# Stick-breaking scan kept as the remaining product, with a floor tile as its mask, and joint transfers for the heads' operands

## The chip, the cores and the metric

The kernel runs on one core of one Trainium2 chip. TensorE (PE) multiplies matrices and transposes, VectorE (DVE) and ScalarE (ACT) work on whole tiles, GpSimd (POOL) and SyncE (SP) mostly issue transfers (DMAs); each engine works through its own instructions in program order. The metric is device time of one execution in microseconds (us), the median of several timed runs.

## What is computed

One decoder block: three gated attention branches side by side (stick-breaking, forgetting, memory cross-attention), merged, projected and added to the input, then a squared-ReLU MLP. Sequence 1024, width 1024, 8 + 8 heads of 64 and 4 memory heads of 128, all in float32. The change is about the stick-breaking branch:

```python
z = jnp.einsum('bhtd,bhsd->bhts', q[:, :, q0:kend], k[:, :, :kend]) * scale
strict = s_idx < t_idx
log_rem = jnp.where(strict, jax.nn.log_sigmoid(-z), 0.0)
after = lax.cumsum(log_rem, axis=3, reverse=True) - log_rem
w = jnp.where(strict, jnp.exp(jax.nn.log_sigmoid(z) + after), 0.0)
outs.append(jnp.einsum('bhts,bhsd->bhtd', w, v[:, :, :kend]))
```

Read from the newest key to the oldest, each key takes the share sigmoid(z) of what is left of a stick, and leaves sigmoid(-z) of it. The weight of key s is what is left before s minus what is left after it. So the sum over keys of weight times value can be written with "what is left" itself and with differences of neighbouring values (`value_step` makes these).

## The kernel before

**Stages.** By the profiled run: up to about 470 us the input is normed and most of the input projection is done; from about 470 to 860 us the attention of all branches runs, with the remaining gate projections and the first of the branch output products put between its pieces on TensorE; the merge, the output projection and the MLP follow (L1871 and on). Every float32 matmul is split in two parts: a high part (a copy on ACT to a shorter format) and a low part (the difference, on DVE), and three products of these are summed.

**What sets the order.** Up to the end of attention the program is written by a planner that runs when the program is built: `Machine` (L184) steps through generators that ask for an engine (`Op`, with a cost in us), a buffer (`Get`) or an event, and writes an engine's next instruction when that engine is free in the plan. So a changed cost or a changed number of buffers moves instructions on all engines. `late` values break ties, and `side` work (the projections) fills TensorE when no attention piece is ready. On the chip each engine keeps the written order, whatever its real durations are.

**Stick-breaking tiles.** `sb_tile` (L812) takes one head and one block of 128 queries, in chunks of up to 512 keys. A chunk gets a buffer `rho` and a PSUM bank, TensorE makes the scores, DVE adds a large number above the diagonal (L834, last chunk only), ACT takes two sigmoids from the scores (L827 into `rho`, L828 into `beta`), and DVE scans from the newest key to the oldest with state = rho * state + beta, which leaves one minus the remaining product (L843). Chunks of the same row wait for the newer one. The queries carry the sign -1 (L1537), so sigmoid(scale * score) is sigmoid(-z). The four `rho` buffers are two tiles of pool `RR`, which has three, lent until the last stick-breaking pair is over (L1609 to L1611, `whole_again`); memory attention and the loads of branch outputs take their tiles from `RR` too.

**Units.** `unit` (L888) runs two such query blocks, then transposes their weights by blocks of 256 keys (`turn`, L917), copies the high part (`pth`, L922, ACT), subtracts for the low part (`ptl`, L924, DVE) and multiplies by the values (L934). Forgetting heads (`fox_tile`, L854) take scores (L869, L870), row maxima (L874) and exponentials (L885) in place of the scan.

**Operands of the heads.** `load_pairs` (L984) fetches queries and keys of two heads at a time from DRAM through POOL's queue, per head and half of the sequence. A stick-breaking head needs its high keys twice, in partitions 0 to 63 and 64 to 127 of one tile, its low keys twice in a second tile, and high and low queries in the two halves of a third: six transfers of 64 rows. A forgetting head has eight with the four rows of forget sums. These tiles come from pool `HT`. The high and low parts lie in two DRAM tensors each (`p_scr`, L119).

**Memory attention and the branch outputs.** `memory` (L573) runs between the other heads. When it is over, `fetched_o` (L1659) loads its output `o_scr` in four tiles of `RR` named `r` (SP's queue), and `bring` (L1679) splits each in two halves (`whi` or `h` on ACT, L1054; `wlo` or `h` on DVE, L1055) for the first branch product. With three tiles, the fourth load waits until the first tile's second half has been split.

Of the kernel before, what the change touches and what calls it, by code (L numbers as in the profile page):

```python
# [21 lines left out]
P = 128  # L22
# [21 lines left out]
def tile_hybrid_block(  # L44
# [58 lines left out]
    sm = C.p.tile([P, 8], F32, tag="sm", name="sm")  # L103
    zero, one = sm[:, 0:1], sm[:, 1:2]
    nc.vector.memset(zero, 0.0)
    nc.vector.memset(one, 1.0)
    gq2, gk2, gmq, gmk, bfg, eps = (sm[:, i:i + 1] for i in range(2, 8))
    nc.vector.memset(eps, EPS * 2.0 ** (2 / 3))

    def root_table():  # L110
# [8 lines left out]
    p_scr = {k: [dram.tile([512, S], F32, name=f"{k}_scr{i}", tag=f"{k}_scr{i}") for i in range(2)]  # L119
             for k in ("sbq", "sbk", "fxq", "fxk", "mq")}  # L120
# [230 lines left out]
    ES, OO, EL, RR, HT, PH, PL, OB, VV, BK, LATER, NONE, RQ = (Places([]) for _ in range(13))  # L351
# [221 lines left out]
    def memory():  # L573
        yield pairs[0].over

        def fetched_q(h, half):
            q = yield Get(HT, 2)

            def issue():
                for t, scr in zip(q, p_scr["mq"]):  # L580
                    nc.gpsimd.dma_start(f32(t), scr[h * P:(h + 1) * P, half * 512:(half + 1) * 512])
            yield from transfer(issue, 2 * P * 512 * 4, 1.1, queue_="POOL")
            q_of[h, half] = q
# [228 lines left out]
    def sb_tile(pair, b, i, beta):  # L812
# [5 lines left out]
        def chunk(ci, c, m, u):  # L818
            rho = yield Get(RQ)
            sc = yield Get(SC)  # L820

# [3 lines left out]

            def sigmoids():
                nc.scalar.activation(rho[:, :u], sc[:, :u], AF.Sigmoid, scale=HD ** -0.5)  # L827
                nc.scalar.activation(beta[:, c:c + u], sc[:, :u], AF.Sigmoid, scale=-HD ** -0.5)  # L828
# [12 lines left out]
            def scan():  # L841
                back = beta[:, c:c + u][:, ::-1]
                nc.vector.tensor_tensor_scan(out=back, data0=rho[:, :u][:, ::-1], data1=back,  # L843
                                             initial=0.0 if last else beta[:, c + u:c + u + 1],
                                             op0=ALU.mult, op1=ALU.add)
            yield Op("DVE", 0.1 + 0.00215 * u, scan, 0.14)
            RQ.put(rho)
# [40 lines left out]
    def unit(pair, b, g, es):  # L888
# [5 lines left out]
        scr, r0 = o_scr[0 if pair.kind == "sb" else 1], (2 * pair.p + b) * HD  # L894
# [5 lines left out]
        def block(k):  # L900
# [11 lines left out]
            def turn():  # L912
# [9 lines left out]
            yield Op("ACT", act_time(512 - lo_c), lambda: nc.scalar.activation(ph[:, lo_c:], tr[:, lo_c:], AF.Copy))  # L922
            pl = yield Get(PL)
            yield Op("DVE", dve_time(512 - lo_c), lambda: nc.vector.tensor_tensor(  # L924
                pl[:, lo_c:], tr[:, lo_c:], f32(ph[:, lo_c:]), ALU.subtract))
# [58 lines left out]
    def load_pairs():  # L984
        yield ready
        for c, pair in enumerate(pairs):
# [5 lines left out]
            for b in range(2):  # L992
# [4 lines left out]
                def halves(half):  # L997
# [7 lines left out]
                    lower, upper, f4 = slice(0, HD), slice(HD, P), slice(HD, HD + 4)  # L1005
# [1715 lines left out]
```

## Time and profile before

| | |
|---|---|
| timed runs | 1685.2, 1686.24, 1687.55 us (median 1686.24) |
| profiled execution | span 1686.7 us from first to last instruction; the page gives no other time for it |
| instructions | 25003 |
| granted TensorE clock, mean | 0.999 |
| DMA | 284.32 MB, mean 169 GB/s |
| ACT busy | 848.9 us (50%) |
| POOL busy | 255.2 us (15%) |

The page gives for each engine the time in which it was busy. A matmul's end is modelled, and matmuls overlap, so TensorE's busy time can hide short waits. In the trace's lists a row is a group of instructions: source line, engine, operation, tiles (out<-in), sizes, count, then busy time, the mean of one in ns, and the idle time before them with what released it. `CUSTOM_DVE_ANT_0` is the row maximum of a forgetting tile with the mask added, and `DVE_READ_ACCUMULATOR2_ANT` reads its result.

### The profile page before, as it was taken

Reading aid. Unit: us, or ns where it says so; the run is one execution under the profiler, and the core shown is the slowest. Engines: PE = TensorE matmul, PEld = TensorE weight load, DVE = VectorE, ACT = ScalarE, POOL = GpSimd, SP = SyncE. Lnnn points to the kernel's source line nnn. Section 1 sums busy time; section 2 is a strip of 40 time slices with the busy share of each in tenths; the row PEclk is TensorE's granted clock in tenths of the full one; section 3 lists DMA queues with packets and bytes.
Section 4 is the critical chain, followed back from the end, with each engine's and each line's share of the span. In section 5 each row is a group of like instructions: output and inputs, shape, how many; then the busy total and the mean of one; then the engine's idle time right before and its main releaser. Section 6 shows DMA issues by size and latency. Waiting matters only on the chain.

```text
span 1686.7 us, 25003 instructions
## 1 busy us (share of the span) xinstructions
PE 1675.3 (99%) x9118; PEld 1432.0 (85%) x9118; DVE 1293.0 (77%) x2079; ACT 848.9 (50%) x1474; POOL 255.2 (15%) x440
## 2 busy tenths in 40 slices
PE   9999999999999999999999999999999999999999
PEld 9998899998888888888888887878888887888887
DVE  7977778855459888867877898987777776688775
ACT  6455555534358888866761446433333344332331
POOL 0000000000253151254400011022111120000000
PEclk9999999999999999999999999999999999999999
DMA  7445434467475365387747542144444484564532
GB/s 245 157 150 182 149 119 150 146 194 243 127 232 161 111 186 151 117 240 224 236 146 245 183 162 100 57 162 155 152 150 137 150 307 171 202 202 143 198 125 75
DMA packets 142221, 284.32 MB, mean 169 GB/s; under 512 B 16913, under 2 KB 53329, under 8 KB 142098
## 3 DMA queue, kind: packets, MB, share of 16 engines
q1 hardware_dynamic: 110562, 183.08, 32.0%
q0 software_dynamic: 31536, 99.64, 19.5%
q8 instruction: 72, 1.18, 0.3%
q14 instruction: 51, 0.42, 0.1%
HBM read 189.83 MB, written 92.83 MB: 168 GB/s over the span
## 4 chain that ended last, share of the span: by engine, by line
PE 92%; DVE 5%; DMA 2%; ACT 1%; issue 1%; SPq 0%; DVEq 0%; ACTq 0%
PE pp L1456 11%; PE pp L1144 10%; PE pp L1981 10%; PE pp L2658 8%; PE sc L1456 7%; PE sc L1144 6%; PE sc L1981 5%; PE sc L2658 4%; PE tr L2658 4%; PE tr L917 4%; PE pv L1456 3%; PE pv L2658 3%; PE tr L1981 2%; PE sc L934 2%; PE pp L934 2%; DVE h L1917 1%
## 5 line engine op out<-in xcount | busy, mean ns | idle before, releaser
L1055 DVE TENSOR_TENSOR wlo<-raw,whi 128x1024 fp32r<-128x1024 f32 (+1 forms) x88 | 107.5, 1222 | 80.2 <-ACT whi L1054 80.0
L1054 ACT ACTIVATE whi<-raw 128x1024 fp32r<-128x1024 f32 (+1 forms) x88 | 93.2, 1059 | 78.8 <-PE pp L1456 32.7
L2658 PE MATMUL pp<-h,sop 128*128 128x512 f32 x540 | 128.4, 396 | 0.0
L2658 PEld LDWEIGHTS pp<-h,sop 128*128 128x128 f32 x540 | 101.6, 188 | 24.4
L1981 PE MATMUL pp<-h,oh 128*128 128x512 f32 x384 | 121.1, 397 | 0.7 <-ACT cu L2066 0.6
L924 DVE TENSOR_TENSOR ptl<-tr,pth 128x512 fp32r<-128x512 f32 (+1 forms) x160 | 99.1, 628 | 24.1 <-ACT pth L922 23.1
L922 ACT ACTIVATE pth<-tr 128x512 fp32r<-128x512 f32 (+1 forms) x160 | 87.4, 556 | 36.0 <-PE sc L934 15.8
L1981 PEld LDWEIGHTS pp<-h,oh 128*128 128x128 f32 x384 | 72.0, 188 | 19.0 <-ACT cu L2066 1.4
L2573 ACT ACTIVATE h<-t 128x2048 fp32r<-128x2048 f32 (+1 forms) x17 | 30.7, 1814 | 110.2 <-DVE t L1917 97.4
L1373 POOL DMA_DIRECT2D raw<-w_in x32 | 24.2, 755 | 395.1 <-DVE wlo L1055 395.1
L1144 PE MATMUL sc<-h,whi 128*128 128x512 f32 (+1 forms) x254 | 77.7, 389 | 0.0
L1456 PE MATMUL pp<-h,whi 128*128 128x512 f32 x248 | 77.5, 394 | 0.0
L1981 PE MATMUL pp<-h,ol 128*128 128x512 f32 x192 | 76.1, 396 | 0.0
L1456 PE MATMUL pp<-whi,h 128*128 128x256 f32 x384 | 71.8, 283 | 0.0
L843 DVE TENSOR_TENSOR_SCAN e<-r,e 128x384 f32<-128x384 f32 (+3 forms) x64 | 66.3, 1044 | 6.9 <-ACT e L828 6.5
L1974 ACT ACTIVATE oh<-raw 128x512 fp32r<-128x512 f32 x64 | 39.4, 625 | 61.8 <-DVE raw L1917 61.8
L2658 PE MATMUL sc<-h,sop 128*128 128x512 f32 x264 | 63.7, 396 | 0.0
L2658 PE MATMUL tr<-h,sop 128*128 128x512 f32 x264 | 63.4, 396 | 0.0
L1917 DVE TENSOR_TENSOR sop<-ur,sop 128x2048 fp32r<-128x2048 f32 (+1 forms) x28 | 61.8, 2211 | 2.0 <-ACT sop L2586 2.0
L917 PE MATMUL tr<-ident,e 128*128 128x128 f32 x416 | 62.7, 273 | 0.0
L1456 PEld LDWEIGHTS pp<-whi,h 128*128 128x128 f32 x384 | 60.2, 188 | 0.0
L2658 PEld LDWEIGHTS sc<-h,sop 128*128 128x128 f32 x264 | 49.6, 188 | 12.3 <-DVE sop L1917 0.5
(558 smaller groups left out, 5087.7 us busy)
## 6 DMA issues: line engine op xcount, KB each, us to landing
ur<-s_scr SPq DMA_DIRECT2D x26, 1024.0 KB
raw<-w_in POOLq DMA_DIRECT2D x42, 512.0 KB, 4.9
raw<-w_up SPq DMA_DIRECT2D x60, 256.0 KB
s_scr<-s POOLq DMA_DIRECT2D x60, 256.0 KB, 2.7
g<-w_down SPq DMA_DIRECT2D x14, 1024.0 KB
s_scr<-cu POOLq DMA_DIRECT2D x48, 256.0 KB, 2.8
h<-sbk_scr POOLq DMA_DIRECT2D x64, 128.0 KB, 3.2
o<-gate_scr SPq DMA_DIRECT2D x32, 256.0 KB
```

The lines of the kernel that those rows point to most:

```text
L843: nc.vector.tensor_tensor_scan(out=back, data0=rho[:, :u][:, ::-1], data1=back, initial=0.0 if last else beta[:, c + u:c + u + 1], op0=ALU ...
L917: nc.tensor.transpose(tr[:, jj * 256 + a * P:jj * 256 + (a + 1) * P], es[a][:, j * P:(j + 1) * P], ident)
L922: yield Op("ACT", act_time(512 - lo_c), lambda: nc.scalar.activation(ph[:, lo_c:], tr[:, lo_c:], AF.Copy))
L924: yield Op("DVE", dve_time(512 - lo_c), lambda: nc.vector.tensor_tensor(pl[:, lo_c:], tr[:, lo_c:], f32(ph[:, lo_c:]), ALU.subtract))
L934: nc.tensor.matmul(pv[0][:, c_:256], pair.v[:, j, b, :], p_[:, jj * 256 + c_:(jj + 1) * 256], start=(k == 0 and n_ == 0 and i == 0), stop= ...
L1054: yield Op("ACT", 0.03 + act_time(m), lambda: nc.scalar.activation(hi, raw, AF.Copy))
L1055: yield Op("DVE", dve_time(m), lambda: nc.vector.tensor_tensor(lo, raw, f32(hi), ALU.subtract))
L1144: nc.tensor.matmul(ps, a_, b_, start=(first and i == 0), stop=(last and i == n - 1))
L1456: nc.tensor.matmul(out_, a_, b_, start=(first and n == 0 and j == 0), stop=(last and n == 3 and j == len(todo) - 1), skip_group_check=True)
L1917: nc.vector.tensor_tensor(out_, a_, b_, op)
L1981: nc.tensor.matmul(ps, w[a_][:, k * P:(k + 1) * P], h[b_][k], start=(first and k == 0 and i == 0), stop=(last and k == 3 and i == 2), skip ...
L2658: nc.tensor.matmul(ps, a_[:, c, qs], b_[:, c, :], start=(kind in ("P1", "P2", "P7") and c == 0 and i == 0), stop=(kind in ("P2", "P4", "P3 ...
```

## The change

1. The second sigmoid, `rho` and the mask addition are gone. ACT writes sigmoid(scale * score) into the weight tile, and the scan runs in place on it: state = max(left * state, floor), from 1.0. The floor of the last chunk is a tile with ones on and above the diagonal, so that the product stays 1 there; for other chunks it is a column of zeros, repeated. The tile now holds the remaining product.
2. The high part of the transposed stick-breaking weights is a copy with -1 added by a bias column (`minus`), the low part a three-operand instruction that adds -1 and subtracts the high part. The differences of the values change their sign.
3. One tile of `RR` is lent instead of two (the floor), and the mask tile `later` loses a column. Two masks are made on POOL instead of one.
4. High and low parts lie in one DRAM tensor. Both copies of a head's keys come in one transfer whose source repeats the rows, and high and low queries in one transfer: three transfers for a stick-breaking head and half, six for a forgetting one, so 80 issues fewer in all. The planner's costs of these issues change with them.

```diff
-    p_scr = {k: [dram.tile([512, S], F32, ...) for i in range(2)]
-             for k in ("sbq", "sbk", "fxq", "fxk", "mq")}
+    p_scr = {k: dram.tile([2, 512, S], F32, ...) for k in ("sbq", "sbk", "fxq", "fxk", "mq")}
...
-    def sb_tile(pair, b, i, beta):
+    def sb_tile(pair, b, i, left):
...
-            rho = yield Get(RQ)
             sc = yield Get(SC)
+            part = left[:, c:c + u]
...
-            def sigmoids():
-                nc.scalar.activation(rho[:, :u], sc[:, :u], AF.Sigmoid, scale=HD ** -0.5)
-                nc.scalar.activation(beta[:, c:c + u], sc[:, :u], AF.Sigmoid, scale=-HD ** -0.5)
...
+            yield Op("ACT", act_time(u), lambda: nc.scalar.activation(
+                part, sc[:, :u], AF.Sigmoid, scale=HD ** -0.5), table=AF.Sigmoid)
+            SC.put(sc)
             last = c + u == n
-            if last:
-                dg = sc[:, u - P:u]
-                yield Op("DVE", 0.22, lambda: nc.vector.tensor_tensor(
-                    dg, dg, holder["later"][:, 385:513], ALU.add))
-            yield Op("ACT", act_time(u, u), sigmoids, table=AF.Sigmoid)
-            SC.put(sc)
             if not last:
                 yield scanned
-
-            def scan():
-                back = beta[:, c:c + u][:, ::-1]
-                nc.vector.tensor_tensor_scan(out=back, data0=rho[:, :u][:, ::-1], data1=back,
-                                             initial=0.0 if last else beta[:, c + u:c + u + 1],
-                                             op0=ALU.mult, op1=ALU.add)
-            yield Op("DVE", 0.1 + 0.00215 * u, scan, 0.14)
-            RQ.put(rho)
+            back = part[:, ::-1]
+            floor = holder["floor"][:, 512 - u:512] if last else zero.to_broadcast([P, u])
+            yield Op("DVE", 0.1 + 0.00215 * u, lambda: nc.vector.tensor_tensor_scan(
+                out=back, data0=back, data1=floor[:, ::-1], initial=1.0 if last else left[:, c + u:c + u + 1],
+                op0=ALU.mult, op1=ALU.max), 0.14)
...
+            yield Op("ACT", act_time(512 - lo_c), lambda: nc.scalar.activation(
+                h_, t_, AF.Identity, bias=minus) if of_sb else nc.scalar.activation(h_, t_, AF.Copy))
...
+            yield Op("DVE", dve_time(512 - lo_c), lambda: nc.vector.scalar_tensor_tensor(
+                pl[:, lo_c:], t_, -1.0, f32(h_), ALU.add, ALU.subtract) if of_sb else nc.vector.tensor_tensor(
+                pl[:, lo_c:], t_, f32(h_), ALU.subtract))
...
+                    def twice(k, src):
+                        nc.gpsimd.dma_start(f32(t[k]), src)
...
                     def keys():
-                        put("k1", lower, ks_[0][rows, cols])
-                        put("k1", upper, ks_[0][rows, cols])
-                        put("k2", lower, ks_[1][rows, cols])
+                        high, low = (ks_[i, rows, cols] for i in range(2))
+                        twice("k1", high.unsqueeze(0).to_broadcast([2, HD, 512]))
                         if fox:
+                            put("k2", lower, low)
                             put("k2", f4, fk_scr[2 * p + b, :, cols])
                         else:
-                            put("k2", upper, ks_[1][rows, cols])
+                            twice("k2", low.unsqueeze(0).to_broadcast([2, HD, 512]))
...
                     def queries():
-                        put("q", lower, qs[0][rows, cols])
-                        put("q", upper, qs[1][rows, cols])
+                        twice("q", qs[:, rows, cols])
...
-        yield Op("DVE", dve_time(512), lambda: nc.vector.tensor_tensor(a, a, b, ALU.subtract))
+        yield Op("DVE", dve_time(512), lambda: nc.vector.tensor_tensor(a, b, a, ALU.subtract))
...
-        halves = [RR.free.popleft() for _ in range(2)]
-        RQ.put(*(t[:, i * 512:(i + 1) * 512] for t in halves for i in range(2)))
-        spawn(whole_again(halves))
-        yield Op("POOL", 1.0, lambda: masked(later))
+        lent_ = RR.free.popleft()
+        holder["floor"] = lent_[:, :512]
+        spawn(whole_again(lent_))
+        yield Op("POOL", 1.0, lambda: masked(holder["floor"], 1.0, -1))
+        yield Op("POOL", 1.0, lambda: masked(holder["later"], -NEG, 0))
```

**What moves.** Before attention and behind it the engines' orders stay as they are, but for the two masks. Three places show the rest. The first is ACT at the start of attention, with the weight tiles `e`, the `rho` tiles `r`, the score banks `pp` and `pv` and a gate tile `o`, before:

```order
L827 ACTIVATE r_4694<-pp_133 128x384
L828 ACTIVATE e_4690<-pp_133 128x384
L827 ACTIVATE r_4694<-pv_140 128x512
L828 ACTIVATE e_4690<-pv_140 128x512
L827 ACTIVATE r_4695<-pp_133 128x512
L828 ACTIVATE e_4691<-pp_133 128x512
L827 ACTIVATE r_4695<-pv_140 128x512
L828 ACTIVATE e_4691<-pv_140 128x512
L1637 ACTIVATE o_4810<-sc_136 128x512
```

and with the change, at the same place:

```order
L826 ACTIVATE e_4686<-pp_129 128x384
L826 ACTIVATE e_4686<-pv_136 128x512
L826 ACTIVATE e_4687<-pp_129 128x512
L826 ACTIVATE e_4687<-pv_136 128x512
L826 ACTIVATE e_4688<-pp_129 128x128
L1632 ACTIVATE o_4798<-sc_132 128x512
```

Each chunk has one row instead of two, and a fifth chunk's sigmoid stands ahead of the first gate's.

The second place is POOL's queue for the first head's operands, key tiles `h` from `sbk_scr` and query tiles from `sbq_scr`, before:

```order
L1004 DMA h_4678<-sbk_scr_84 64x512 x2
L1004 DMA h_4677<-sbk_scr_85 64x512 x2
L1004 DMA h_4681<-sbk_scr_84 64x512 x2
L1004 DMA h_4680<-sbk_scr_85 64x512 x2
L1004 DMA h_4679<-sbq_scr_82 64x512
L1004 DMA h_4679<-sbq_scr_83 64x512
L1004 DMA h_4676<-sbq_scr_82 64x512
L1004 DMA h_4676<-sbq_scr_83 64x512
```

and with the change:

```order
L1000 DMA h_4674<-sbk_scr 128x1x512
L1000 DMA h_4673<-sbk_scr 128x1x512
L1000 DMA h_4677<-sbk_scr 128x1x512
L1000 DMA h_4676<-sbk_scr 128x1x512
L1000 DMA h_4675<-sbq_scr 128x1x512
L1000 DMA h_4672<-sbq_scr 128x1x512
```

Twelve transfers of 64 rows have become six of 128 rows.

The third place is DVE in the forgetting heads, where the memory attention's output is split for the first branch product. The tiles `r` are the loaded outputs, `wlo` and `h` beside them their low parts, `ptl` the low part of attention weights, `e,st` a row maximum and `st` its reading. Before, the last rows ahead of the fourth load's first split, which is the last row here:

```order
L924 TENSOR_TENSOR ptl_4802<-tr_139,pth_4800 128x384
L1055 TENSOR_TENSOR wlo_168<-raw_170,whi_167 128x1024
L1055 TENSOR_TENSOR h_7212<-r_4694,h_7212 128x512
L1055 TENSOR_TENSOR h_7213<-r_4695,h_7213 128x512
L924 TENSOR_TENSOR ptl_4801<-tr_138,pth_4799 128x384
L1055 TENSOR_TENSOR h_7213<-r_4695,h_7213 128x512
L924 TENSOR_TENSOR ptl_4802<-tr_139,pth_4800 128x512
L874 ISA e_4690,st_7404<-pv_140,sm 128x512
L874 ISA st_7404 128x1
L874 ISA e_4690,st_7404<-pp_133,later_4697 128x384
L874 ISA st_7404 128x1
L1055 TENSOR_TENSOR h_7214<-r_4696,h_7214 128x512
```

With the change, the last rows ahead of the same split:

```order
L1049 TENSOR_TENSOR h_7408<-r_4690,h_7408 128x512
L917 TENSOR_TENSOR ptl_4789<-tr_134,pth_4787 128x384
L917 TENSOR_TENSOR ptl_4790<-tr_135,pth_4788 128x512
L917 TENSOR_TENSOR ptl_4789<-tr_134,pth_4787 128x512
L863 ISA e_4686,st_7496<-pp_129,sm 128x512
L863 ISA st_7496 128x1
L863 ISA e_4686,st_7496<-pv_136,later_4693 128x384
L863 ISA st_7496 128x1
L917 TENSOR_TENSOR ptl_4790<-tr_135,pth_4788 128x384
L872 TENSOR_TENSOR st_7496<-st_7496 128x1
L1049 TENSOR_TENSOR wlo_164<-raw_166,whi_163 128x1024
L1049 TENSOR_TENSOR h_7409<-r_4692,h_7409 128x512
```

In both, the fourth load takes the tile of the first (`r_4696`, now `r_4692`), which its second `wlo` split sets free: that split stands 13 rows ahead of the last row before, and 18 rows ahead with the change. On TensorE the last transposes of memory attention have moved behind more of the forgetting heads, and the first branch product starts some 280 matmuls later.

More of the change, by code (lines that the diff above doesn't have):

```diff
@@ L102, in tile_hybrid_block @@
     make_identity(nc, ident)
-    sm = C.p.tile([P, 8], F32, tag="sm", name="sm")
-    zero, one = sm[:, 0:1], sm[:, 1:2]
+    sm = C.p.tile([P, 9], F32, tag="sm", name="sm")
+    zero, one, minus = sm[:, 0:1], sm[:, 1:2], sm[:, 8:9]
     nc.vector.memset(zero, 0.0)
     nc.vector.memset(one, 1.0)
+    nc.vector.memset(minus, -1.0)
     gq2, gk2, gmq, gmk, bfg, eps = (sm[:, i:i + 1] for i in range(2, 8))
@@ L893, in unit @@
         pair.read(b, g)
-        scr, r0 = o_scr[0 if pair.kind == "sb" else 1], (2 * pair.p + b) * HD
+        of_sb = pair.kind == "sb"
+        scr, r0 = o_scr[0 if of_sb else 1], (2 * pair.p + b) * HD
         js = list(range(2 * g + 1, -1, -1))
@@ L1023, in load_pairs @@
                 (k1_, q1_), (k0_, q0_) = halves(1), halves(0)
-                evs = [spawn(transfer(k0_, 4 * HD * 2048, 1.6, queue_="POOL"), -20.0), spawn(transfer(k1_, 4 * HD * 2048, 1.6, queue_="POOL"), -20.0),
-                       spawn(transfer(q1_, (3 if fox else 2) * HD * 2048, 1.2, queue_="POOL"), -20.0),
-                       spawn(transfer(q0_, (3 if fox else 2) * HD * 2048, 1.2, queue_="POOL"), -20.0)]
+                evs = [*(spawn(transfer(k_, 4 * HD * 2048, 1.5 if fox else 1.0, queue_="POOL"), -20.0) for k_ in (k0_, k1_)),
+                       *(spawn(transfer(q_, (3 if fox else 2) * HD * 2048, 1.5 if fox else 0.5, queue_="POOL"), -20.0) for q_ in (q1_, q0_))]
                 if b == 0:
@@ L1545, in out_ @@
             def out_():
-                for scr, t_ in zip(p_scr[u], (hi, lo)):
+                for scr, t_ in zip((p_scr[u][0], p_scr[u][1]), (hi, lo)):
                     nc.sync.dma_start(scr[rows, cols], t_)
```

30 lines of the change are left out of this document (14 added, 16 removed).

## The prediction

> **What bounds the kernel.** I read the page first: the engines' shares and the chain of work that ended last.
>
> ```profile
> PE 1675.3 (99%) x9118; PEld 1432.0 (85%) x9118; DVE 1293.0 (77%) x2079; ACT 848.9 (50%) x1474; POOL 255.2 (15%) x440
> ...
> PE 92%; DVE 5%; DMA 2%; ACT 1%; issue 1%; SPq 0%; DVEq 0%; ACTq 0%
> ```
>
> TensorE is busy for 1675.3 of 1686.7 us and makes 92% of the chain. By the order of the built program the change leaves TensorE the same 9120 matmuls and transposes; only those of the attention stage (about 470 to 900 us) stand in another order. Work taken from ACT, DVE or POOL is therefore worth only what it takes from TensorE's idle time in that stage. The list of waits, for TensorE and these 430 us, has one row:
>
> ```profile
> PE pv L869 <- DVE st L874: 1.5, 1, 1.5
> ```
>
> The stage in stretches (us, TensorE, its weight loads, DVE, ACT and POOL busy with instruction counts, granted clock, DMA share, GB/s):
>
> ```profile
> 500.00:550.00 50.00, 50.00 (x313) 44.12 (x312) 46.59 (x80) 40.79 (x93) 16.84 (x30) 1.00 0.59 178
> ...
> 700.00:750.00 50.00, 48.53 (x280) 41.35 (x278) 33.33 (x89) 35.11 (x75) 20.69 (x39) 0.97 0.73 213
> ```
>
> From 500 to 550, with DVE at 46.59 of 50, TensorE never stands. It stands once, between 700 and 750, and there the clock has a dent. Closer:
>
> ```profile
> 741.00:743.00 2.00, 0.53 (x3) 0.30 (x2) 1.83 (x5) 1.96 (x5) 0.00 (x0) 1.00 0.98 323
> 743.00:748.00 5.00, 5.00 (x22) 3.97 (x21) 2.50 (x11) 3.09 (x9) 0.00 (x0) 0.66 0.92 324
> ```
>
> TensorE is idle for 2.00 - 0.53 = 1.47 us, and in the 5 us behind it runs at 0.66 of the clock, which loses 5 x 0.34 = 1.70 us. The stall costs 1.47 + 1.70 = **3.17 us**. Its cause, in order of time (start, length, engine, idle before and its releaser):
>
> ```profile
> 731.58 0.33 SPq L1663 DMA_DIRECT2D r<-o_scr  x1
> ...
> 740.50 0.63 ACT L1054 ACTIVATE h<-r 128x512 fp32r<-128x512 f32 x1 [3.58 <-DMA r<-o_scr]
> ...
> 741.17 0.69 DVE L1055 TENSOR_TENSOR h<-r,h 128x512 fp32r<-128x512 f32 x1 [2.32 <-ACT h L1054]
> ...
> 741.85 0.68 DVE L874 CUSTOM_DVE_ANT_0 e<-pv,sm 128x512 f32<-128x512 f32 x1
> ...
> 742.59 0.50 PE L869 MATMUL pv<-h,h 128*128 128x512 f32 x1 [1.47 <-DVE st L874]
> ```
>
> The fourth load of memory-attention output landed 8.9 us after its issue. ACT, then DVE, stood at its split; behind them stood the row maxima that free a PSUM bank for the next fox score.
>
> **The change, part by part.** Busy time from 470 to 900 us of the second sigmoid (L828, ACT), the mask addition (L834, DVE) and the scan (L843, DVE), one row each:
>
> ```profile
> 470.00:900.00 430.00, 48.39 (x96) 1.00 0.62 186
> ...
> 470.00:900.00 430.00, 18.15 (x64) 1.00 0.62 186
> ...
> 470.00:900.00 430.00, 91.89 (x96) 1.00 0.62 186
> ```
>
> ACT loses 48.4 us, and four fewer table loads at 1.283 us take 5.1 more; DVE loses 18.2 us. All of it lies beside a full TensorE, so each counts as 0. What operations become instead:
>
> ```profile
> L827 ACT ACT_TABLE_LOAD x7 | 9.0, 1283 | 0.1
> ...
> L843 DVE TENSOR_TENSOR_SCAN e<-r,e 128x512 f32<-128x512 f32 x40 | 50.4, 1264 | 3.5 <-ACT e L828 3.1
> L1323 DVE TENSOR_TENSOR_SCAN sn<-sn,sm 8x512 f32<-8x512 f32 x2 | 2.4, 1208 | 0.0
> L924 DVE TENSOR_TENSOR ptl<-tr,pth 128x512 fp32r<-128x512 f32 x96 | 65.1, 682 | 18.4 <-ACT pth L922 17.7 <-PE pp L824 0.3
> L1539 DVE SCALAR_TENSOR_TENSOR sn<-sn,sn 128x512 fp32r<-128x512 f32 x12 | 8.1, 686 | 1.0 <-ACT sn L1538 0.9
> L922 ACT ACTIVATE pth<-tr 128x512 fp32r<-128x512 f32 x96 | 57.2, 599 | 14.2 <-PE sc L934 11.0 <-PE pp L934 2.4 <-PE tr L917 0.5
> L738 ACT ACTIVATE sn<-tr,sm 128x512 fp32r<-128x512 f32 x26 | 17.5, 684 | 10.8 <-PE tr L732 10.4
> ```
>
> The scan wrote in place before (1264 ns), and one with a repeated zero column took 1208 ns. A scan with a maximum is not in the trace. The lower end is 682 ns, a plain pass of this size, the upper twice 1264 ns; I take 1264, the same line's row. The 80 low parts as three-operand instructions cost 686 instead of 682 ns, 0.3 us in all. The 80 high parts with a bias column are bounded by 599 (no column) and 684 ns (a column as scale); I take 599, since they read the same tile, and at the upper end they add 6.8 us to an ACT that lost 53. All this is hidden; it would cost TensorE only in stretches where DVE has no spare, and it has 50 - 46.6 us in the fullest one even before the mask additions go.
>
> The joint transfers take 80 issues from POOL, at 527 ns each (64 rows) against 545 ns for 128 rows:
>
> ```profile
> L1004 POOL DMA_DIRECT2D h<-sbk_scr x64 | 33.3, 527 | 97.1 <-PE pv L151 29.6 <-DVE wlo L1055 19.1 <-PE pp L824 13.2
> L581 POOL DMA_DIRECT2D h<-mq_scr x16 | 8.6, 545 | 38.8 <-PE pp L824 14.8 <-DVE ob L963 13.7 <-PE pv L823 7.0
> ...
> h<-sbk_scr POOLq DMA_DIRECT2D x64, 128.0 KB, 3.2
> h<-mq_scr POOLq DMA_DIRECT2D x16, 256.0 KB, 3.9
> ...
> 694.70 0.54 POOL L1004 DMA_DIRECT2D h<-fq_scr  x1
> ...
> 705.70 0.40 PE L869 MATMUL pp<-h,h 128*128 128x512 f32 x1
> ```
>
> POOL is no bound, so its 42 us count as 0. A landing time matters only where TensorE has to wait for it: the medians are 3.2 us for 64 rows and 3.9 us for 128. In the tightest set of head operands that I found, the last issue is at 694.70 and the set's first product at 705.70, 11 us later. I take 3.9 us for a joint transfer, which 11 us cover. Its upper end is worked out with the rivals.
>
> **The one place where the path changes** is the stall. In the order, DVE's work between the release of the fourth tile (the end of the second `wlo` split of the first tile) and the fourth split grows from 12 rows to 17; the ends of both stretches stand in the section on the change. Their durations:
>
> ```profile
> L924 DVE TENSOR_TENSOR ptl<-tr,pth 128x384 fp32r<-128x384 f32 x64 | 35.0, 546 | 5.7 <-ACT pth L922 5.4
> L1055 DVE TENSOR_TENSOR h<-r,h 128x512 fp32r<-128x512 f32 x16 | 10.7, 685 | 3.4 <-ACT h L1054 3.3
> L1055 DVE TENSOR_TENSOR wlo<-raw,whi 128x1024 fp32r<-128x1024 f32 x19 | 23.1, 1214 | 6.9 <-ACT whi L1054 6.9
> L874 DVE CUSTOM_DVE_ANT_0 e<-pv,sm 128x512 f32<-128x512 f32 x31 | 21.3, 687 | 6.6 <-PE pv L870 6.3
> L874 DVE CUSTOM_DVE_ANT_0 e<-pp,later 128x384 f32<-128x384 f32 x8 | 4.4, 549 | 0.1
> L874 DVE DVE_READ_ACCUMULATOR2_ANT st<- 128x1 f32 x96 | 8.0, 83 | 0.0
> ```
>
> Before: four splits (2.74), two low parts of 384 and one of 512 (1.77), a weight split (1.21), two maxima with their reads (1.40): 7.1 us, after which DVE stood for 2.32. It could have gone on at 741.17 - 731.58 = 9.6 us after the issue. Of the change: four splits (2.74), two low parts of 384 and four of 512 (3.82), the weight split (1.21), two maxima (1.40): 9.2 us, and two small instructions besides. If the load lands as before, DVE's wait falls from 2.3 us to about 0.4 or less. TensorE bore 2.32 - 1.47 = 0.85 us of such a wait without standing, so the stall goes: **-3.17 us**. What is late next there is the same split again, once the landing passes 8.9 + 0.85 - 0.4, some 9.4 us. Nothing else in the stage waits.
>
> The sum: 1686.7 - 3.2 = 1683.5 us by the profiled span. The page gives no time around the span; the three timed runs (1685.2 to 1687.55, median 1686.24) lie about it, so I take the difference from the median: 1686.24 - 3.17 = **1683.1 us**, 0.19% faster. That is just inside the 0.2% (3.4 us: under 1682.9 or over 1689.6) that a measurement of this kernel can tell from no change.
>
> **The rivals.** (1) The stall stays, or one like it stands elsewhere. The landing of 8.9 us came with the DMA share at 0.98 (the stretch at 741), and the head loads that crowd it are still there, in fewer issues. Then 1686.2. For it: the cover worked out above is tight. Against it: no other wait in 430 us.
>
> (2) Slower: a joint transfer runs on two DMA engines instead of 16, because its source begins with a dimension of two (two copies, or high and low).
>
> ```profile
> q0 software_dynamic: 31536, 99.64, 19.5%
> ```
>
> POOL's queue moved 99.64 MB in 0.195 x 16 x 1686.7 us of engine time, 18.9 GB/s per engine. Half of 256 KB on one engine then takes 131072 B / 18.9 GB/s = 6.9 us against 0.9 us on sixteen: a landing of about 3.9 + 6.0 = 9.9 us, and up to 17 where other transfers take half of each engine. It decides from 11 us, the cover of the tightest set. If three sets between the loads of the memory attention each stand 2 us and lose 1.7 us of clock, that is 11.1 us: 1683.1 + 11.1 = 1694.2. For it: the sources do lead with two. Against it: most sets have more cover, and nothing in the trace shows a large transfer on few engines. [...]
>
> (3) The dent in the clock does not come from the idle time and turns up elsewhere. Then only 1.47 us go: 1684.8. For it:
>
> ```profile
> 1022.00:1026.00 4.00, 2.46 (x16) 1.82 (x15) 3.86 (x12) 3.09 (x8) 0.00 (x0) 1.00 0.84 222
> ```
>
> Here 1.54 us of idle time within 4 us left the clock at 1.00. [...]
>
> (4) Faster than forecast: waits hidden in the modelled ends of matmuls.
>
> ```profile
> L934 PE MATMUL sc<-pth,v 128*128 128x256 f32 x136 | 41.3, 320 | 0.0
> L934 PE MATMUL sc<-ptl,v 128*128 128x256 f32 x136 | 35.8, 280 | 0.0
> ```
>
> The high part's product is 40 ns longer than the low part's; if that were waiting for ACT, 136 x 0.04 = 5.4 us could go: 1677.7. Against it: it follows the transposes, and these stay as many.
>
> (5) The scan with a maximum takes twice as long. DVE would pass its 3.4 spare us in 50 and become the bound of 200 us; far slower, over 1700.
>
> That the change doesn't do what it says is excluded for its counts: the built order has no second sigmoid and no mask addition.
>
> **How the numbers follow.** Forecast (stall gone, none new, 1682.3 to 1684.3): 0.43. (1) 0.20. (2) 0.19, three quarters of it over 1689.6. (3) 0.06. (4) 0.08. (5) 0.04. Faster by over 0.2%: (4) and somewhat under half of the forecast's own spread, 0.26. Slower: three quarters of (2), and (5), 0.18. Within: 0.56. The range goes from 1681.5, which leaves out (4), to 1694.0, which takes in most of (2) and leaves out (5) and its rest. The forecast with (1) and (3) alone lies between 1682.3 and 1687.
>
> **What would show it.** Right: from 470 to 900 us TensorE has no wait in its list, the clock stays at 1.00, ACT's busy time is some 53 us and DVE's some 18 us smaller, and the span is 3 us shorter. Wrong by (1): a wait on a split of `r` again. Wrong by (2): joint transfers that land after 9 us or more, and TensorE's scores waiting for them. Wrong by (5): scans over 1.6 us. I would be most surprised by a gain of over 5 us, since there is no idle time for it.

## The result: slower by 1.6%, and the profile after

The changed kernel takes 1712.37 us (median of 4 runs, 1711.9 to 1716.57) against 1685.9 us before: a ratio of 1.0161, 95% interval 1.0149 to 1.0173. The forecast was 1683.1, with a range to 1694.0. Its direction was that of rival (2), its size more than twice that rival's. The profiled execution spans 1710.5 us and its run took 1712.3 us, so 1.8 us lie around the span.

The page of the changed kernel, its shares of busy time:

```profile
PE 1684.8 (98%) x9118; PEld 1436.6 (84%) x9118; DVE 1279.1 (75%) x2016; ACT 817.4 (48%) x1374; POOL 240.4 (14%) x362
```

Its view of transfers (packets of all queues, POOL's queue, and two groups of issues with size and median time to landing):

```profile
DMA packets 176778, 284.57 MB, mean 166 GB/s; under 512 B 51473, under 2 KB 87889, under 8 KB 176658
...
q0 software_dynamic: 66096, 99.92, 21.6%
...
h<-sbk_scr POOLq DMA_DIRECT2D x32, 256.0 KB, 12.7
...
h<-sbq_scr POOLq DMA_DIRECT2D x16, 256.0 KB, 13.1
```

The joint transfers land after some 13 us, where 64 rows took 3.2, and POOL's queue moves the same megabytes in twice the packets. ACT and DVE do less, as was meant. TensorE pays. Its list of waits from 470 to 900 us had one row before; now it has nine, and these are the seven of 1 us or more (engine, line, what it waited for: us in total, times, longest):

```profile
PE pp L858 <- DVE st L863: 6.3, 1, 6.3
PE tr L907 <- DVE ptl L917: 2.8, 2, 2.4
PE tr L907 <- ACT ob L616: 1.6, 1, 1.6
PE pv L823 <- DMA h<-sbq_scr: 1.4, 1, 1.4
PE tr L907 <- DVE ptl L916: 1.3, 1, 1.3
PE pv L823 <- ACT e L826: 1.0, 1, 1.0
PE tr L614 <- DVE ptl L917: 1.0, 1, 1.0
```

Windows of the changed kernel (length; TensorE, its weight loads, DVE, ACT, POOL busy; granted clock, DMA share, GB/s):

```profile
470.00:900.00 430.00, 413.23 (x2533) 361.07 (x2532) 314.27 (x639) 288.22 (x614) 125.83 (x183) 0.98 0.69 175
757.52:760.93 3.41, 3.41 (x13) 3.02 (x14) 1.42 (x4) 1.15 (x4) 0.49 (x1) 0.50 1.09 255
818.96:829.20 10.24, 6.43 (x25) 5.94 (x26) 6.95 (x19) 5.16 (x13) 4.20 (x6) 0.50 0.87 259
```

TensorE is idle for 430 - 413.23 = 16.8 us of the stage, where it was 1.5, and works (3.41 + 6.43) us at half the clock, which loses 4.9 us where it lost 1.7. That makes 15.3 + 3.2 = 18.5 of the 23.8 us between the profiled spans. Only 1.4 us of the list above name a joint transfer. The longest wait came about like this, in the changed kernel's timeline:

```profile
805.42 1.11 SPq L1667 DMA_DIRECT2D r<-l_scr  x2
807.42 0.33 SPq L618 DMA_DIRECT2D l_scr<-ob  x1
811.93 0.55 POOL L997 DMA_DIRECT2D h<-fq_scr  x1 [4.59 <-DMA h<-fxk_scr]
820.80 1.23 DVE L1670 TENSOR_TENSOR r<-r,r 128x1024 f32<-128x1024 f32 x1 [6.87 <-DMA r<-l_scr]
821.01 0.38 ACT L946 ACTIVATE ob<-pp 128x256 f32<-128x256 f32 x1 [7.15 <-DMA l_scr<-ob]
822.02 0.68 DVE L863 CUSTOM_DVE_ANT_0 e<-pp,sm 128x512 f32<-128x512 f32 x1
822.76 0.47 PE L858 MATMUL pp<-h,h 128*128 128x128 f32 x1 [6.25 <-DVE st L863]
```

Two loads that SyncE had issued by 806.5 us let DVE go on at 820.8, and a small store of 807.42 us frees ACT's buffer at 821.0. Neither is a joint transfer, or on the same queue. DVE stands at `r`, and the row maximum that TensorE needs is queued behind it. POOL meanwhile waits 4.6 us for one of its own transfers before it can issue the next.

### The profile page after: what moved, and what is told of

The parts are those of the page before. It is cut to its first block, busy times and chain, and to the rows that moved or that the text cites. A ratio compares the mean times of both kernels' runs of the same rounds, so it can differ in the third digit from the quotient of the medians.

```text
span 1710.5 us, 24661 instructions
## 1 busy us (share of the span) xinstructions
PE 1684.8 (98%) x9118; PEld 1436.6 (84%) x9118; DVE 1279.1 (75%) x2016; ACT 817.4 (48%) x1374; POOL 240.4 (14%) x362
## 2 busy tenths in 40 slices
DMA packets 176778, 284.57 MB, mean 166 GB/s; under 512 B 51473, under 2 KB 87889, under 8 KB 176658
## 4 chain that ended last, share of the span: by engine, by line
PE 84%; DMA 7%; DVE 5%; ACT 1%; issue 1%; POOL 1%; SPq 0%; ACTq 0%; POOLq 0%; DVEq 0%
PE pp L1450 11%; PE pp L1976 10%; PE pp L1138 8%; PE pp L2653 8%; PE sc L1450 7%; PE sc L1976 5%; PE sc L1138 4%; PE sc L2653 4%; PE tr L2653 4%; DMA raw<-w_in 3%; PE pv L1450 3%; PE tr L907 3%; PE pv L2653 3%; PE tr L1976 2%; PE sc L927 2%; PE pp L927 1%
## 5 line engine op out<-in xcount | busy, mean ns | idle before, releaser
L907 PEld LDWEIGHTS tr<-ident,e 128*128 128x128 f32 x416 | 51.1, 143 | 17.2 <-DVE ptl L917 3.8
L917 DVE TENSOR_TENSOR ptl<-tr,pth 128x384 fp32r<-128x384 f32 (+1 forms) x80 | 50.3, 633 | 20.3 <-ACT pth L914 20.0
L913 ACT ACTIVATE pth<-tr,sm 128x384 fp32r<-128x384 f32 (+1 forms) x80 | 50.7, 646 | 25.4 <-PE pp L927 13.0
## 6 DMA issues: line engine op xcount, KB each, us to landing
h<-sbk_scr POOLq DMA_DIRECT2D x32, 256.0 KB, 12.7
```

The costliest lines, as they stand in the source:

```text
L907: nc.tensor.transpose(tr[:, jj * 256 + a * P:jj * 256 + (a + 1) * P], es[a][:, j * P:(j + 1) * P], ident)
L917: pl[:, lo_c:], t_, -1.0, f32(h_), ALU.add, ALU.subtract) if of_sb else nc.vector.tensor_tensor(
```

## Experiments

**Theory T**: a joint transfer runs on two DMA engines; it lands late, holds up POOL's queue, and the transfers of all queues that have a share on these two engines. **Rivals**: O, the new order of the planner leaves too little time whatever the transfers do; S, the new scan costs the time. Four kernels tell them apart; in all, the code shown replaces the lines of the changed kernel, or of the kernel before where that is said. All ran on one chip, with the kernel before at 1685.96 us.

Two issues of 64 rows, costs and so the order of the changed kernel:

```diff
-                        twice("k1", high.unsqueeze(0).to_broadcast([2, HD, 512]))
+                        put("k1", lower, high)
+                        put("k1", upper, high)
...
-                        twice("q", qs[:, rows, cols])
+                        put("q", lower, qs[0, rows, cols])
+                        put("q", upper, qs[1, rows, cols])
```

> The changed kernel with each joint transfer issued as two transfers of 64 rows again; the planner's costs stay, so TensorE, DVE and ACT keep the order of the changed kernel. Theory T (a joint transfer runs on two DMA engines, lands after 12 us and blocks POOL's queue and the others): packets under 512 B fall from 51473 to about 15600, a load of sbk_scr lands after 3 to 4.5 us, POOL's waits for its own DMAs between 450 and 900 us fall from some 100 us to some 25, TensorE's idle time there from 16.8 to under 3 us, time 1682 to 1689 us. Theory O (the new order itself leaves the loads too little time): most of the 16.8 us stay, 1698 to 1712 us.

Rows slowest, halves inside (the pattern goes row by row and has a row's two halves one after the other; in the changed kernel the halves are slowest):

```diff
-                        twice("k1", high.unsqueeze(0).to_broadcast([2, HD, 512]))
+                        twice("k1", high.unsqueeze(1).to_broadcast([HD, 2, 512]))
...
-                        twice("q", qs[:, rows, cols])
+                        twice("q", qs[:, rows, cols].rearrange("i r n -> r i n"))
```

> The changed kernel with its joint transfers as they are in number and bytes, but the rows as the slowest dimension of the source and the two halves inside it (the tile's 128 rows then alternate between the halves, in queries and keys alike). Theory T: the 35840 small packets are gone (under 512 B about 15600), 256 KB land after 3.5 to 5 us, time 1682 to 1689 us. Rival (a transfer of 256 KB that repeats or gathers its source is slow whatever the order of its dimensions): landings over 9 us and 1700 us or more.

The kernel before with `keys`, `queries` and their costs as in the changed kernel, and the scratch tensors joined for it; the lines of the scan stay as they were:

```diff
-                        put("k1", lower, ks_[0][rows, cols])
-                        put("k1", upper, ks_[0][rows, cols])
+                        twice("k1", high.unsqueeze(0).to_broadcast([2, HD, 512]))
...
-                        put("q", lower, qs[0][rows, cols])
-                        put("q", upper, qs[1][rows, cols])
+                        twice("q", qs[:, rows, cols])
```

> The kernel before, with the changed kernel's joint transfers (halves slowest) and their planner costs, and none of the change of the scan. Theory T: as slow as the changed kernel, 1698 to 1716 us, 35840 small packets more than before, landings of 9 us and over. Theory S (the new scan, its masks or the two-operand high and low parts cost the time): 1683 to 1689 us.

The changed kernel with `keys`, `queries` and the costs of the kernel before (shown: the costs; the issues are those of the first diff):

```diff
-                evs = [*(spawn(transfer(k_, 4 * HD * 2048, 1.5 if fox else 1.0, queue_="POOL"), -20.0) for k_ in (k0_, k1_)),
+                evs = [spawn(transfer(k0_, 4 * HD * 2048, 1.6, queue_="POOL"), -20.0), spawn(transfer(k1_, 4 * HD * 2048, 1.6, queue_="POOL"), -20.0),
...
```

> The change of the scan alone: transfers of 64 rows and the planner costs of the kernel before. Theory T: no long stall from 470 to 900 us, 1682 to 1688 us; the stall of 3.2 us of the kernel before may stay or go with the order. Theory S: 1698 us or more.

Measured: 1693.11 us with two issues (ratio 1.0042, 1.0029 to 1.0054), 1691.27 with rows slowest (1.0032, 1.0020 to 1.0045), 1717.77 for the old scan with joint transfers (1.0189, 1.0175 to 1.0203), 1688.72 for the new scan alone (1.0019, 1.0010 to 1.0028). All four lie above the range that theory T gave, the run with two issues about halfway to that of theory O. So the joint transfers are not the whole cost; what is left is taken up below. The view of transfers of the run with rows slowest:

```profile
DMA packets 140938, 284.29 MB, mean 168 GB/s; under 512 B 15633, under 2 KB 52049, under 8 KB 140818
...
h<-sbk_scr POOLq DMA_DIRECT2D x32, 256.0 KB, 4.1
...
h<-sbq_scr POOLq DMA_DIRECT2D x16, 256.0 KB, 6.0
...
h<-fxk_scr POOLq DMA_DIRECT2D x16, 256.0 KB, 4.3
...
h<-fq_scr POOLq DMA_DIRECT2D x16, 8.0 KB, 4.6
```

The same 80 transfers of the same bytes, in the same order on every engine, land after 4.1 to 6.0 us (medians by tensor) instead of 10.4 to 13.1 when only the order of the transfer's dimensions differs: 21.1 us of time. The small packets hint at the number of engines. The changed kernel has 51473 - 15633 = 35840 more of them, 448 for each of 80 joint transfers, and 448 = 14 x 32: as if two engines got 32 pieces of data each, and each of the other 14 got 32 empty ones (this queue's records show 256 KB as 64 pieces of 4 KB, and the extra packets hold 8 bytes each: 35840 of that size in the trace, none in that of the kernel before). The records don't name the engine, so this is a reading of the counts; the small packets of further runs fit it (29969 and 30481, below). The times of the packets fit it too. When the first joint transfers of the changed kernel run, from 463.8 to 465.0 us, never more than three of the queue's pieces of 4 KB are in flight, and 53 GB/s move from 464.00 to 464.50; in the kernel before, with the first transfers of 64 rows, up to 17 are in flight, and 238 GB/s move from 462.00 to 462.50. In the changed kernel two pieces are in flight at 465.0 us, four at 465.3, six at 465.5 and eight at 466.0, when five joint transfers have been issued and nothing else in that queue: they grow by twos, so by the same reading a transfer takes other engines than the one before it.

S falls: the old scan with these transfers is no faster than the new one. O falls as the main cause, but not altogether. In both runs with fast transfers one wait remains, here that with rows slowest (waits, then the timeline):

```profile
PE pp L858 <- DVE st L863: 1.9, 1, 1.9
```

```profile
803.86 1.23 DVE L1670 TENSOR_TENSOR r<-r,r 128x1024 f32<-128x1024 f32 x1 [2.50 <-DMA r<-l_scr]
805.82 0.33 PE L858 MATMUL pp<-h,h 128*128 128x128 f32 x1 [1.88 <-DVE st L863]
```

It is the place of the 6.3 us wait, in its undisturbed size: the new order brings the load of `l_scr` close to its use. SyncE had issued the two loads by 794.0 us here, and DVE went on 9.9 us later; in the changed kernel it was 14.3 us. With the old costs it is gone:

```profile
470.00:900.00 430.00, 429.81 (x2634) 376.74 (x2633) 332.57 (x665) 290.81 (x616) 143.36 (x260) 1.00 0.63 186
```

That is the window of the run with the new scan alone: 0.2 us idle in the stage, full clock. Yet its 11 runs take 2.8 us longer than the kernel before, which no wait explains. Its products are slower (the line's own answer, the kernel before first, then the new scan alone: duration in ns min/median/max, first and last start in us):

```profile
L2658 PE MATMUL pp<-h,sop x540: 392/394/399, 1391.1 to 1679.5; 128*128 128x512 f32 x180
```

```profile
L2652 PE MATMUL pp<-h,sop x540: 392/397/400, 1390.2 to 1679.6; 128*128 128x512 f32 x180
```

The same 540 products of the MLP, far behind the change and with no wait between them, take 289.4 us from first to last start instead of 288.4. What can reach them is line 103 of the kernel: `sm`, the tile that holds columns such as `minus`, grew from 8 columns to 9, and in the built programs the tiles allocated behind it start at other addresses (no trace shows an address). **Theory A** says that this is the cost. Three kernels test it and what follows for the best version, a fourth takes theory T further; the kernel before had 1686.16 us beside them.

```diff
-    sm = C.p.tile([P, 8], F32, tag="sm", name="sm")
+    sm = C.p.tile([P, 9], F32, tag="sm", name="sm")
```

> The kernel before with one number changed: the tile of columns sm has 9 columns instead of 8, the ninth unused. Every engine's order is unchanged; the tiles allocated behind sm lie 32 bytes further (on multiples of 64 bytes where they were 32 above one). Theory A (the kernels with the new scan run each product some tenths of a nanosecond slower because of these addresses; the run with the new scan alone had no stall and full clock, and was yet 2.8 us slower than before): 1687.5 to 1689.5 us. Rival (it comes from the new scan's instructions or from nothing that is the kernel's): 1685 to 1687 us.

The new scan alone, with wider `sm`; the candidate has this line too, besides rows slowest and the old costs:

```diff
-    sm = C.p.tile([P, 9], F32, tag="sm", name="sm")
+    sm = C.p.tile([P, 17], F32, tag="sm", name="sm")
```

> The run with the new scan alone (old transfers, old costs, 1688.7 us), with sm of 17 columns: the tiles behind it lie 32 bytes above a multiple of 64 again. Theory A: 1684.5 to 1687 us, 2 to 3 us less than without it, and as that run has no stall, below the kernel before. Rival: 1688 to 1689.5 us as without it.

> A candidate for the best: the new scan, joint transfers with the rows slowest, the planner costs of the kernel before (whose order had no stall with the new scan), sm of 17 columns. If the stall of the other run with rows slowest belongs to its order, and theory A holds: no TensorE wait over 0.5 us between 470 and 900 us, 1684 to 1687 us. If the stall belongs to the joint transfers even so: 1687 to 1691 us.

The changed kernel with the halves slowest in the forgetting pairs (`fox`) alone:

```diff
-                        twice("q", qs[:, rows, cols])
+                        twice("q", qs[:, rows, cols] if fox else qs[:, rows, cols].rearrange("i r n -> r i n"))
```

and `keys` in the same way:

> The changed kernel with the rows slowest in the stick-breaking pairs' 48 joint transfers, the halves slowest still in the forgetting pairs' 32; order unchanged. Theory T: 32 x 448 = 14336 small packets more than with none, so 29969 under 512 B; TensorE's waits before 660 us go (3.3 us of idle), those behind it (12 us of idle and 4.9 us of half clock) stay: 1704 to 1710 us, loads of sbk_scr after 4 to 5 us and of fxk_scr after 9 to 13 us. If the stick-breaking pairs' transfers were what delays the rest: under 1698 us.

Measured: 1688.97 us for the kernel before with nine columns (1.0017, 1.0008 to 1.0026), 1685.40 for the new scan with 17 (0.9995, 0.9986 to 1.0004), 1686.41 for the candidate (1.0003, 0.9994 to 1.0011), 1711.44 with the forgetting pairs alone on two engines (1.0145, 1.0130 to 1.0161). One number, with every engine's instructions in the same order, costs 2.8 us. The products of the MLP, in the kernel before with nine columns and in the new scan with 17:

```profile
L2658 PE MATMUL pp<-h,sop x540: 392/397/400, 1389.7 to 1679.1; 128*128 128x512 f32 x180
```

```profile
L2652 PE MATMUL pp<-h,sop x540: 387/394/398, 1388.6 to 1676.8; 128*128 128x512 f32 x180
```

They take 289.4 us with nine columns, and 288.2 with 17. Against the run that differs in this number alone (1688.72, on another chip), the 17 columns save 3.3 us. So theory A holds as far as a shift of 32 bytes goes. With nine columns both, new and old scan stand at 1.0019 and 1.0017 of the kernel before: alone the new scan changes nothing that can be measured. The candidate's one wait is the place that the forecast was about, now 1.0 us long, where at most 0.5 was expected; it is no better than the kernel before.

With two engines for the forgetting pairs alone, the small packets are 29969, as expected (32 x 448 more), and the time is above the expected 1704 to 1710: 32 of the 80 transfers cost nearly as much as all (1.0145 against 1.0161). The waits before 660 us are gone, and those behind it grew:

```profile
PE pp L858 <- DMA h<-fxq_scr: 6.5, 1, 6.5
PE tr L907 <- DVE ptl L917: 4.5, 2, 2.5
PE tr L614 <- DVE ptl L917: 3.5, 2, 2.5
```

Here the longest wait is for a joint operand itself. Is the loss the lateness of these operands, or what the transfers do to others? The next kernel has both sorts apart; its neighbours close what theory A left open (the kernel before: 1685.67 us).

```diff
                     def twice(k, src):
                         nc.gpsimd.dma_start(f32(t[k]), src)
+                        if fox:
+                            both = (ks_ if k == "k1" else qs)[:, rows, cols]
+                            nc.gpsimd.dma_start(extra[((2 * p + b) * 2 + half) * 2 + (k == "q")], both)
```

> The run with the rows slowest everywhere (1691.3 us, 15633 small packets), and behind each of the forgetting pairs' 32 joint transfers an extra transfer of the same 256 KB, halves slowest, into a scratch tensor that nothing reads; it adds 32 issues on POOL (some 26 us). So nobody waits for the data of a transfer on two engines, but POOL's queue and the two engines carry as many as in the run with the forgetting pairs alone on two engines (1711.4 us). Theory C (the others' transfers behind the two engines and POOL's waits for its own DMAs make most of the loss): 29969 small packets, 1702 to 1715 us, late landings of h<-fq_scr and of ordinary loads again. Theory L (the loss comes from TensorE waiting for the joint operands themselves): 1690 to 1697 us.

> The run with the new scan alone and 17 columns (1685.4 us), with sm of 25 columns: the tiles behind it lie on multiples of 64 bytes again, another 32 further. Theory A (32 bytes above a multiple of 64 is fast, a multiple of 64 slow): 1688 to 1690 us. Rival (what counts is the place within 128 bytes or more, and 9 columns are a bad one): 1684 to 1687 us.

> The changed kernel with sm of 17 columns instead of 9 and nothing else, every engine's order unchanged. If the term for the addresses (2.8 us) and that of the joint transfers add up: 1708.5 to 1710.5 us. If the slower products only fill time in which TensorE waits anyway: 1711 to 1713 us.

Measured: 1716.84 us with the extra transfers (1.0179, 1.0163 to 1.0194), 1687.30 with 25 columns (1.0008, 0.9999 to 1.0017), 1711.22 for the changed kernel with 17 columns (1.0151, 1.0137 to 1.0165). The first diff is put on the run with rows slowest, with `extra` declared beside the other scratch tensors; the other two runs have `sm` of 25 and of 17 columns. The run with the extra transfers, its view of transfers, then TensorE's waits:

```profile
DMA packets 157834, 292.79 MB, mean 171 GB/s; under 512 B 30481, under 2 KB 66897, under 8 KB 157714
...
h<-fxk_scr POOLq DMA_DIRECT2D x16, 256.0 KB, 8.2
extra<-fxk_scr POOLq DMA_DIRECT2D x16, 256.0 KB, 9.4
...
h<-fq_scr POOLq DMA_DIRECT2D x16, 8.0 KB, 9.0
```

```profile
PE tr L908 <- DVE ptl L918: 8.0, 4, 4.0
PE pv L824 <- ACT e L827: 4.1, 1, 4.1
PE pp L860 <- DMA h<-fq_scr: 2.9, 1, 2.9
```

Theory C holds against theory L. Nothing reads what an extra transfer brings, and no load that is waited for has its halves slowest; yet those land twice as late (8.2 us for keys that took 4.3, 9.0 for a load of only 8 KB that took 4.6), and 25.6 us are lost against the run without the extra ones. POOL alone waits for extra transfers: between 450 and 900 us it stands 56 us for earlier ones before it issues more. So later issues and slower landings both have a part, and these runs don't separate them. These also add 8.4 MB and 32 issues; that this alone does it is unlikely, since rows slowest against two issues (80 issues more) differ by only 1.8 us, but was not tried apart. The small packets are 14848 more: 32 x 448, and 16 for each transfer that is added. In the same way, two issues instead of rows slowest (80 transfers more) gave 16913 instead of 15633.

With 25 columns, again on multiples of 64 bytes, the time came out between the two theories: 1.9 us above 17 columns but 1.4 below nine, on three chips. The 540 products of the MLP have 288.2 us from first to last start and a median of 394 ns with 25 columns, as with 17, where nine columns have 289.4 us and 397 ns. So the place within 64 bytes alone does not seem to decide, and the rule stays open. The changed kernel with 17 columns lies just inside the range that was expected if slower products only fill time in which TensorE waits. It takes 1.2 us less than with nine, by medians on different chips, where 2.8 were expected if the terms add; its range (1709.67 to 1712.7) overlaps that of the changed kernel, so this stays open too. In the table, each ratio is to the kernel before in the same set of runs (1685.9 to 1686.16 us).

| Kernel | Scan | Transfers | Costs | `sm` | us | Ratio |
|---|---|---|---|---|---|---|
| before | old | 64 rows | old | 8 | 1685.9 | 1 |
| changed | new | two engines | new | 9 | 1712.37 | 1.0161 |
| two issues | new | 64 rows | new | 9 | 1693.11 | 1.0042 |
| rows slowest | new | rows slowest | new | 9 | 1691.27 | 1.0032 |
| old scan, joint transfers | old | two engines | new | 8 | 1717.77 | 1.0189 |
| new scan alone | new | 64 rows | old | 9 | 1688.72 | 1.0019 |
| before, nine columns | old | 64 rows | old | 9 | 1688.97 | 1.0017 |
| new scan, 17 columns | new | 64 rows | old | 17 | 1685.40 | 0.9995 |
| candidate | new | rows slowest | old | 17 | 1686.41 | 1.0003 |

No version beats the kernel before by more than the measurement can tell; the new scan with 17 columns is nearest to it.

## Why the prediction was wrong, step by step

**The joint transfers: the step that failed.** "I take 3.9 us for a joint transfer, which 11 us cover" was wrong twice. The landing was 12.7 us; rival (2) gave 9.9 to 17 for it, from two engines, which no row of the kernel before showed and the packet counts now fit, and I gave that a chance of 0.19, in part because "nothing in the trace shows a large transfer on few engines". No large transfer of the kernel before has such a source, so its silence was no evidence. Both sorts of source gave the 448 small packets: the two real halves in each of the 32 extra transfers (14848 = 32 x 448 + 32 x 16), the repeated rows and the real halves together in the 80 joint ones (35840 = 80 x 448). That these stand for two engines stays a reading: the records name none. Then the price: I worked it out from the cover of the heads' own sets, 11.1 us. From rows slowest to halves slowest it is 21.1 us (1712.37 - 1691.27), and the extra transfers show that it does not need a late operand. Other loads of POOL's queue landed after 8.2 us instead of 4.3 beside them, and in the changed kernel SyncE's loads of `l_scr` let DVE go on after 14.3 us instead of 9.9. So the cover that mattered was not that of the heads' own sets alone: the longest wait was for `l_scr`, for which DVE stood 2.5 us even with rows slowest. The stated range ended at 1694.0, just short of this rival's own 1694.2.

**The stall of 3.17 us: a mis-sized term.** It was in the profiled execution, and I subtracted it from the median. With 1.8 us around a span, the profiled run took some 1688.5 us, above the slowest of the three timed; 1686.24 corresponds to a span of some 1684.4. The profiled run of the kernel before with nine columns, in the same order, has a mean clock of 1.000. A step of 3.41 us at half clock takes 0.001 off the mean granted clock of the whole run, and the profiled execution has 0.999; of 57 later timed runs of the kernel before, 52 have 1.000. What most runs had to lose there was thus far less than 3.17 us. The mechanism was right: in both runs with fast transfers the new order has no wait there.

**Rival (1), "one like it stands elsewhere", came too**: the load of `l_scr`, with 1.9 us of wait and a step at half clock behind it. The new costs with rows slowest, against the old costs with 64 rows, are 1691.27 - 1688.72 = 2.6 us; with 64 rows in both, the costs alone are 1693.11 - 1688.72 = 4.4 us.

**A term I never saw: the ninth column.** It is one line of the diff, and the sum has no term for it and gives no reason. It is 2.8 us.

The three together are 21.1 + 2.6 + 2.8 = 26.5 us, where 1712.37 - 1685.9 = 26.5; that they sum is by construction of the chain of kernels, except that the last is measured on the kernel before.

**What was right.** Work off ACT and DVE is worth nothing here: new and old scan differ by 0.02% with nine columns both. Rival (5) fell, the scan with a maximum costs as much as the one with an addition (1264). Of the high parts with a bias I took the lower end, and it was the upper (684):

```profile
L834 DVE TENSOR_TENSOR_SCAN e<-e,sm 128x512 f32<-128x512 f32 x32 | 40.6, 1270 | 2.7 <-ACT e L826 1.9
L913 ACT ACTIVATE pth<-tr,sm 128x512 fp32r<-128x512 f32 x48 | 33.1, 689 | 19.1 <-PE pp L927 12.3 <-PE sc L927 6.4
```

DVE's busy time fell by 13.9 us instead of 18 and ACT's by 31.5 instead of 53; these high parts take some 7 us of ACT's difference back. The rest is mostly that I added up rows, and neighbours overlap on ACT: before, one first sigmoid starts at 560.00 us and lasts 0.60, and its second starts at 560.50. Summed by instruction, ACT's work fell by 48.2 us. Rival (3) fell: the runs with no long wait (the new scan alone, 17 columns, the candidate) keep full clock through the stage. Nothing of rival (4) was seen.

## What to carry to other kernels

Put the long dimension slowest when you join two transfers: with a leading dimension of two, repeated or real, these landed after 10.4 to 13.1 us (medians by tensor) instead of 4.1 to 6.0, and joining them that way cost 21.1 us, far more than the 80 issues it saved on a POOL that is no bound. Price a slow transfer by the tightest load of any queue that runs beside it, not by who reads its data. And before a stall of a profile is subtracted from a median, ask whether the median run has it; and when a tile grows by one column, test the new addresses alone.

## What the runs showed of the hardware

**Addresses.** With the ninth column, which puts the tiles 32 bytes further, the median of a 128x512 product in the MLP was 397 ns instead of 394, and the kernel took 2.8 us more of 1686; with 25 columns the median was 394 again. That it is the addresses rests on the edit, which changes nothing else that is known; which addresses are good is open.

**The clock.** In the traces of the two kernels the granted clock changed at the edges of a grid of 3.413 us: half clock for one step of it, from 743.75 to 747.16 us, in the kernel before, and in the changed kernel for one from 757.52 to 760.93 and three from 818.96 to 829.20. Within one step at full clock (in both traces, and in the attention of seven further runs), 1.88 us or more of TensorE's idle time (that least in the run with rows slowest, in the step from 803.56; its mean clock from 806 to 811 us is 0.66) were followed by a step at half clock each time, 1.45 us (the changed kernel, from 622.89 to 624.34) or less never. Amounts between were followed by either: 1.47 us in the kernel before, at 740.33, and 1.75 with the extra transfers, at 758.41, by half clock; 1.52 in the kernel before, at 1023.64, 1.56 with the forgetting pairs alone, at 812.44, and 1.87 with the extra transfers, at 659.42, by full clock. What decides between the two is open. By these figures a stall of 2 us within one step costs an estimated 3.7 us, 2 and half of the next 3.41.
